# A hybrid encoder block: two thirds of the convolution's taps as ScalarE products, and six pairs instead of four by seven products in four groups

## The chip, the core and the metric

The kernel runs on one core of one Trainium2 chip. A core has a matrix engine (TensorE, PE in the profile, with its weight loads as PEld), a vector engine (VectorE, DVE), an activation engine (ScalarE, ACT), a general engine (GpSimd, POOL) and a queue engine (SyncE, SP) that here only issues transfers. Each works through its own instructions in order, and they wait for each other by semaphores. The metric is device time in microseconds (us) of one execution; the times given are medians.

## What is computed

One layer of a streaming encoder on 256 rows of 4096 columns, all in float32:

```python
proj = rms_norm(h, norm_in_g) @ w_in             # 4096 -> 7 x 2048: q, k, v, z_a, a_c, g_c, z_c
y_a  = rms_norm(chunked_attention(q, k, v, table)) * silu(z_a)
u    = a_c * sigmoid(g_c)                        # 256 rows x 2048 channels
u    = causal_depthwise_conv(u, w_dw) + b_dw     # 31 taps, one filter for each channel
y_c  = rms_norm(silu(layer_norm(u)) @ w_pw + b_pw) * silu(z_c)
h    = h + concat(y_a, y_c) @ w_out
h    = h + sigmoid(rms_norm(h) @ w_ple_gate + b) * (p @ w_ple)
out  = rms_norm(h)
```

The change touches the depthwise convolution and the products that make a_c, g_c, q, k and v.

## The kernel before

**Precision.** Each float32 matrix is split into a high part (a cast to fp32r) and a low part (the rest), and each product of two blocks is three: high by high, low by high, high by low. For a weight tile of 128 x 1024 that means one cast on ScalarE (line 204: `wh`, `uh`) and one subtraction on VectorE (line 205: `wl`, `ul`). Weight tiles arrive in five buffers, the parts of plain tiles have three buffers each, those of sums two.

**A group.** `mixed_product` makes two blocks of 512 output columns for both halves of the 256 rows, four accumulators, over the 4096 inner rows, which are sixteen pairs of 128-row blocks. A *plain* pair takes 2 blocks x 2 row halves x 2 column blocks x 3 = 24 products of 128x512. A pair *by seven products* (a Strassen-Winograd step) takes 7 x 3 = 21, but needs sums of its weight blocks. They are made by VectorE: two for `ua` (lines 467 and 468) and two for `ub` (474 and 475), and both results are split like weights. A pair marked `*` does just that. A pair marked `+` has its `ua` summed by two transfers, one on SP's queue and an accumulating one on GpSimd's (lines 420 and 421), and keeps only 474 and 475 on VectorE. The left side needs sums of the activations too ("combinations"). Those of pairs 8 and 10 are made while a group runs, in `more_combinations`, and are used by sevens 8 and 10.

The order of a group's pairs is a list written out by hand:

```python
early     = units("1 3 5 0+ 7 9 2+ 11 13 4+ 15 8 6+ 10 12 14")       # four sevens
early_six = units("1 3 5 0+ 7 2* 9 4+ 11 6* 13 8+ 15 10* 12 14")     # six sevens
```

After the last seven, VectorE adds up the helper accumulators (lines 513 to 516); after the last pair it scales the four accumulators into `z` (line 538), and TensorE transposes the result.

**Order of the groups.** conv 0, conv 1 (each makes a_c and g_c for 512 channels), q0/k0, v0/v1, attention 0, conv 2, q1/k1, attention 1, conv 3, q2/k2, q3/v2, attention 2, layer norm, k3/v3, attention 3, and then the pointwise, output and embedding products. Conv 2 and conv 3 use `early_six`; conv 1, q0/k0, v0/v1, q1/k1 and q2/k2 use `early`; q3/v2 has five sevens.

**The convolution.** At the end of each conv group the gated values are transposed into `uT` (four blocks of 128 channels x 256 rows), and `glu_conv` puts the taps into a queue of small tasks, `later`: for each of the four blocks, 31 instructions on VectorE, each of which takes `uT` shifted by some rows, multiplies by one column of weights and adds to `cv` (line 724; the unshifted one, with the offset, is line 720). The shifted tap k covers 226 + k columns, so 241 on average. After each pair of a group, `fill(n)` takes n tasks from the queue, by the lists `early_fills` (64 in all) and `six_fills` (63).

**What sets the order on an engine.** The instructions are traced in program order. Then they are put into each engine's queue by that order among those that are ready; so an instruction that needs nothing may come much earlier than it was traced. `queued_behind(made)` puts what is traced inside it behind the given instruction on the same engine. `recent` holds the newest pair of cast and subtraction. Tiles of one tag share a fixed number of slots: "hd" has five of 128 x 1024 (`uT`, the bias tables, `kT`, v), "stage" two, "act" eight.

Of the kernel before, what the change touches and what calls it, by code (L numbers as in the profile page):

```python
# [10 lines left out]
F32 = mybir.dt.float32  # L11
F32R = mybir.dt.float32r
AF = mybir.ActivationFunctionType
ALU = mybir.AluOpType
AX = mybir.AxisListType

P = 128
# [8 lines left out]
def hybrid_block(  # L26
# [305 lines left out]
    early_five = units("1 3 5 0+ 7 9 2+ 11 4* 13 6+ 15 8* 10 12 14")  # L332
    early_six = units("1 3 5 0+ 7 2* 9 4+ 11 6* 13 8+ 15 10* 12 14")

    early_fills = (5, 6, 1, 5, 6, 1, 5, 6, 1, 5, 6, 1, 2, 5, 5, 4)
    six_fills = (6, 6, 1, 5, 1, 5, 1, 5, 1, 5, 1, 5, 1, 6, 7, 7)
    norm = units("1 3 5 7 9 11 0+ 13 2* 15 4+ 8 6* 10 12 14")
    norm_fills = (7, 8, 8, 8, 6, 4, 2, 3, 2, 3, 2, 2, 0, 6, 5, 5)
    final = units("1 0* 3 2* 5 4* 6* 7 8* 9 10* 12* 11 13 14 15")
# [378 lines left out]
    def conv_tap(cv, uT, i, b, k):  # L718
# [4 lines left out]
        else:  # L723
# [2 lines left out]
                cv[:, i, PAD - k :], ALU.mult, ALU.add,  # L726
            )

    def more_combinations(pair):

        if pair in (7, 9):
            c = (pair + 1) // 2
            xS[2 * c] = act.tile([P, 2, 2, T], F32R, tag="act", name="comb_x"), 0
            later.extendleft(reversed(combinations(c)))

    def glu_conv(c):
        if c == 0:
            sg, gate = scaled_pair(
                w_in0, o_a, o_g - o_a, first, r_x, (1,), begin=first_pairs
            )  # L740
        else:
            sg, gate = scaled_pair(
                w_in0, o_a + c * NB, o_g - o_a,
                *((early, r_x, early_fills) if c == 1 else (early_six, r_x, six_fills)),
                ahead=more_combinations if c == 2 else None,
            )
        for h in range(NH):
            nc.scalar.activation(gate[:, h, :], gate[:, h, :], AF.Sigmoid)
            tt(sg[:, h, :], sg[:, h, :], gate[:, h, :], ALU.mult)
        uT = spool.tile([P, 4, T], F32, tag="hd", name="uT", bufs=5)  # L750
        for pair in range(2):
            pt = tmp_psum()
            for i in range(2):
                for h in range(NH):
                    b = 2 * pair + i
                    nc.tensor.transpose(
                        pt[:, i * T + h * P : i * T + (h + 1) * P],
                        sg[:, h, b * P : (b + 1) * P],
                        ident,
                    )  # L760
            nc.scalar.copy(
                uT[:, 2 * pair : 2 * pair + 2, :], pt.rearrange("q (i t) -> q i t", t=T)
            )
        cv = act.tile([P, 4, T], F32, tag="act", name="cv")
        for i in range(4):
            for k in reversed(range(TAPS)):
                later.append(partial(conv_tap, cv, uT, i, 4 * c + i, k))
        conv.append(cv)


# [184 lines left out]
    def heads(*parts, order=None, fills=early_fills, **kw):  # L955

        cols = [o + g * NB for o, g in parts]
        tiles = scaled_pair(
            w_in0, cols[0], cols[1] - cols[0], order or early, r_x, fills,
            homes=[home if o == o_v else dict(tag="stage") for o, _ in parts], **kw  # L960
        )
        for (o, g), t in zip(parts, tiles):
            if o == o_v:
                vs[g] = t
            else:
                (queries_of if o == o_q else keys_of)(g, t)
# [6 lines left out]

    n_g = H // GH
    assert n_g == CW // NB == 4
    glu_conv(0)
    glu_conv(1)
    load_bias(0)
    heads((o_q, 0), (o_k, 0))
    heads((o_v, 0), (o_v, 1))  # L980
    attention(0)
    glu_conv(2)
    load_bias(1)
    heads((o_q, 1), (o_k, 1))
    attention(1)
    glu_conv(3)
    load_bias(2)
    heads((o_q, 2), (o_k, 2))
    heads((o_q, 3), (o_v, 2), order=early_five)
    attention(2)  # L990
    layer_norm_swish()
    load_bias(3)
# [359 lines left out]
```

## Time and profile before

| | us |
|---|---|
| median of three runs | 2029.58 |
| lowest and highest | 2027.98, 2029.75 |
| the profiled execution | 2028.23 |
| its span, first to last instruction | 2026.5 |
| PE, DVE, ACT busy in the span | 2010.8, 1903.4, 1215.0 |
| granted TensorE clock | 0.998 |

The profile is one execution. Its page lists busy times, the chain of work that ended last and the costliest groups of instructions; the trace behind it can be asked for stretches of time, single lines and the order of instructions. A group's row gives line, engine, operation, the tile written and those read, shape and count, then busy time and mean duration in ns, and after the second bar the idle time just ahead of these instructions and what ended it. Products overlap in the record (each lasts about 0.39 us but the next starts earlier), so a busy PE isn't PE at its full rate: the distance between their starts tells more than the busy share.

### The profile page before, as it was taken

The numbers are of one execution on the slowest core, as the hardware profiler recorded it, in microseconds if no ns is written. First come the engines' busy times: TensorE is split into PE (matmuls) and PEld (weight loads), VectorE is DVE, ScalarE is ACT, GpSimd is POOL, SyncE is SP. The second block draws the span as 40 slices with busy tenths as digits, with TensorE's granted clock in tenths as the row PEclk, the third lists the DMA queues.
The fourth block names the chain that finished last, engine by engine and source line by source line (L and its number), as shares of the span: only waits on it lengthen the run. The fifth ranks groups of instructions, "written<-read, shape, count | busy, mean of one in ns | idle before, by whom it ended". The sixth has DMA issues, their size and how long they took to land.

```text
span 2026.5 us, 26195 instructions
## 1 busy us (share of the span) xinstructions
PE 2010.8 (99%) x9073; PEld 1654.4 (82%) x9073; DVE 1903.4 (94%) x2708; ACT 1215.0 (60%) x1583; POOL 46.9 (2%) x50
## 2 busy tenths in 40 slices
PE   9999999999999999999999999999999999999997
PEld 7888888888888888788888888888888888888876
DVE  7999999889999997888899999999999999999998
ACT  7655545655655555776556556666665666655555
POOL 0000000000000000000000000000000000000000
PEclk9999999999999999999999999999999999999999
DMA  8787878678678867456666666676666656666765
GB/s 295 222 238 234 255 217 250 177 247 240 188 221 246 252 198 241 156 177 209 196 208 207 208 204 211 208 239 210 203 211 197 208 194 201 208 218 207 231 207 180
DMA packets 171168, 436.70 MB, mean 215 GB/s; under 512 B 13966, under 2 KB 17182, under 8 KB 171034
## 3 DMA queue, kind: packets, MB, share of 16 engines
q1 hardware_dynamic: 161952, 417.93, 63.9%
q0 software_dynamic: 8432, 16.25, 4.8%
q8 instruction: 71, 1.16, 0.2%
q10 hardware_dynamic: 650, 0.84, 0.1%
q14 instruction: 63, 0.52, 0.1%
HBM read 430.77 MB, written 4.19 MB: 215 GB/s over the span
## 4 chain that ended last, share of the span: by engine, by line
PE 95%; DVE 3%; issue 1%; ACT 1%; DMA 0%; POOLq 0%; POOL 0%; ACTq 0%; SPq 0%; DVEq 0%
PE acc L385 73%; PE acc_P L385 17%; PE tmp_ps L170 1%; DVE cv L724 1%; PE acc L229 1%; DVE wl L205 1%; PE tmp_ps L893 0%; PE tmp_ps L877 0%; PE tmp_ps L911 0%; PE tmp_ps L916 0%; PE acc L373 0%; ACT wh L204 0%; PE tmp_ps L892 0%; DVE ul L205 0%; DMA xin<-in_x_dram 0%
## 5 line engine op out<-in xcount | busy, mean ns | idle before, releaser
L385 PE MATMUL acc<-wh,big_t 128*128 128x512 f32 x4154 | 1283.3, 391 | 0.6 <-DVE y_c L1043 0.4
L204 ACT CAST wh<-wt 128x1024 fp32r<-128x1024 f32 (+1 forms) x737 | 710.1, 974 | 523.3 <-PE acc L385 364.3
L385 PEld LDWEIGHTS acc<-wh,big_t 128*128 128x128 f32 x4154 | 777.0, 188 | 160.8 <-DVE y_c L1043 0.9
L205 DVE TENSOR_TENSOR wl<-wt,wh 128x1024 fp32r<-128x1024 f32 (+1 forms) x737 | 817.4, 1122 | 39.9 <-ACT wh L204 33.6
L385 PE MATMUL acc<-wl,big_t 128*128 128x512 f32 x2077 | 801.9, 391 | 0.1
L385 PEld LDWEIGHTS acc<-wl,big_t 128*128 128x128 f32 x2077 | 389.5, 188 | 82.5 <-DVE wl L205 1.8
L204 ACT CAST uh<-ua 128x1024 fp32r<-128x1024 f32 x174 | 182.9, 1052 | 91.1 <-DVE ua L468 46.3
L205 DVE TENSOR_TENSOR ul<-ua,uh 128x1024 fp32r<-128x1024 f32 x174 | 212.0, 1219 | 9.6 <-ACT uh L204 8.1
L724 DVE SCALAR_TENSOR_TENSOR cv<-uT,dw,cv 128x250 f32<-128x250 f32 (+19 forms) x480 | 203.6, 464 | 1.1
L385 PE MATMUL acc_P<-uh,big_t 128*128 128x512 f32 x528 | 161.8, 392 | 0.0
L204 ACT CAST uh<-ub 128x1024 fp32r<-128x1024 f32 x92 | 96.8, 1052 | 95.5 <-DVE ub L475 79.2
L205 DVE TENSOR_TENSOR ul<-ub,uh 128x1024 fp32r<-128x1024 f32 x92 | 112.2, 1220 | 6.7 <-ACT uh L204 5.6
L385 PEld LDWEIGHTS acc_P<-uh,big_t 128*128 128x128 f32 x528 | 98.0, 188 | 23.2 <-ACT uh L204 3.7
L385 PE MATMUL acc_P<-ul,big_t 128*128 128x512 f32 x264 | 101.3, 392 | 0.0
L467 DVE TENSOR_TENSOR ua<-wt 128x512 f32<-128x512 f32 x102 | 69.9, 685 | 17.3 <-DMA wt<-in_w_in_dram 10.7
L385 PE MATMUL acc<-uh,big_t 128*128 128x512 f32 x266 | 82.5, 390 | 0.0
L385 PE MATMUL acc_P<-wh,big_t 128*128 128x512 f32 x266 | 82.1, 389 | 0.0
L468 DVE TENSOR_TENSOR ua<-wt 128x512 f32<-128x512 f32 x102 | 69.6, 683 | 4.3 <-DMA wt<-in_w_in_dram 3.6
L385 PE MATMUL acc_P<-uh,comb_t 128*128 128x512 f32 x228 | 70.1, 390 | 0.1
L475 DVE TENSOR_TENSOR ub<-ub,wt 128x512 f32<-128x512 f32 x92 | 63.0, 685 | 0.8
L474 DVE TENSOR_TENSOR ub<-ua,wt 128x512 f32<-128x512 f32 x92 | 62.9, 683 | 0.3
L385 PEld LDWEIGHTS acc_P<-ul,big_t 128*128 128x128 f32 x264 | 49.3, 188 | 12.5 <-DVE ul L205 2.0
(243 smaller groups left out, 1485.5 us busy)
## 6 DMA issues: line engine op xcount, KB each, us to landing
wt<-in_w_in_dram SPq DMA_DIRECT2D x416, 512.0 KB, 4.5
wt<-in_w_out_dram SPq DMA_DIRECT2D x128, 512.0 KB, 4.3
wt<-in_w_ple_gate_dram SPq DMA_DIRECT2D x128, 512.0 KB, 4.2
wt<-in_w_pw_dram SPq DMA_DIRECT2D x32, 512.0 KB, 4.8
ua<-in_w_in_dram SPq DMA_DIRECT2D x31, 512.0 KB, 4.3
ua<-in_w_in_dram POOLq DMA_DIRECT2D x31, 512.0 KB, 8.7
wt<-in_w_in_dram SPq DMA_DIRECT2D x31, 256.0 KB, 2.8
hc<-in_x_dram SPq DMA_DIRECT2D x8, 512.0 KB, 4.7
```

Of the source, the lines that this page charges most:

```text
L170: nc.tensor.transpose(pt[:, i * T + h * P : i * T + (h + 1) * P], src[:, h, b] if len(src.shape) == 4 else src[:, h, b * P : (b + 1) * P], ...
L204: nc.scalar.copy(wh[:, :kc, :], wt[:, :kc, :]),
L205: nc.vector.tensor_tensor(wl[:, :kc, :], wt[:, :kc, :], wh[:, :kc, :].bitcast(F32), ALU.subtract),
L229: nc.tensor.matmul(acc, a, b[:, k, :], start=kb == 0 and kind == 0, stop=kb == kblocks - 1 and kind == 2,)
L385: nc.tensor.matmul(banks[name], a, b, start=name not in begun, stop=final and ends[name] == n and kind == 2 and not (left and name in "P2 ...
L467: plus(ua[:, 0], w0[:, 0], w0[:, 1])
L468: plus(ua[:, 1], w0[:, 1], w1[:, 1])
L474: plus(ub[:, 0], ua[:, 0], w1[:, 1])
L475: plus(ub[:, 1], ub[:, 0], w1[:, 0])
L724: nc.vector.scalar_tensor_tensor(cv[:, i, PAD - k :], uT[:, i, : T + k - PAD], dw[:, b, k : k + 1], cv[:, i, PAD - k :], ALU.mult, ALU.add,)
```

## The change

Four parts, all between conv 1 and attention 2:

- q0/k0, v0/v1, q1/k1 and q2/k2 use `early_six` in place of `early`: two more sevens each, and three `+` and three `*` in place of four `+`.
- Of each convolution's 30 shifted taps, every third stays as it was (k = 0, 3, ..., 27; four VectorE instructions each). The other twenty become a *wide tap*: four products on ScalarE, one for each block, into a tile `wu`, and one addition on VectorE for all four blocks. The products are queued behind the newest weight cast (`recent[0]`). `wu` has two tiles in turn, which are taken from the "hd" or "stage" slots, newly for each group.
- A convolution is now 64 tasks (4 + 20 wide + 40 narrow) in place of 124, taken by shorter lists: 37 for `early_fills`, 36 for `six_fills`.
- The combinations for pairs 8 and 10 are made in conv 1's group in place of conv 2's.

```diff
-    early_fills = (5, 6, 1, 5, 6, 1, 5, 6, 1, 5, 6, 1, 2, 5, 5, 4)
-    six_fills = (6, 6, 1, 5, 1, 5, 1, 5, 1, 5, 1, 5, 1, 6, 7, 7)
+    early_fills = (3, 3, 1, 3, 3, 1, 3, 3, 1, 3, 3, 1, 1, 3, 3, 2)
+    six_fills = (3, 3, 1, 3, 1, 3, 1, 3, 1, 3, 1, 3, 1, 3, 3, 3)
...
+    weighted = []
+
+    def weighted_in(*homes):
+
+        weighted[:] = homes
+
+    def wide_tap(cv, uT, b, k):
+
+        if not hasattr(weighted[0], "rearrange"):
+            weighted[:] = [spool.tile([P, 4, T], F32, name="wu", **kw) for kw in weighted]
+        weighted.append(weighted.pop(0))
+        n = T + k - PAD
+        with queued_behind(recent[:1]):
+            for i in range(4):
+                nc.scalar.activation(
+                    weighted[0][:, i, :n], uT[:, i, :n], AF.Identity, scale=dw[:, b + i, k : k + 1]
+                )
+            tt(cv[:, :, PAD - k :], cv[:, :, PAD - k :], weighted[0][:, :, :n], ALU.add)
...
-                ahead=more_combinations if c == 2 else None,
+                ahead=more_combinations if c == 1 else None,
...
-        for i in range(4):
-            for k in reversed(range(TAPS)):
-                later.append(partial(conv_tap, cv, uT, i, 4 * c + i, k))
+        def taps(k, blocks):
+            later.extend(partial(conv_tap, cv, uT, i, 4 * c + i, k) for i in blocks)
+
+        taps(PAD, range(4))
+        for k in range(0, PAD, 3):
+            for n in range(2):
+                later.append(partial(wide_tap, cv, uT, 4 * c, k + 1 + n))
+                taps(k, (2 * n, 2 * n + 1))
...
+    stage, six = dict(tag="stage"), dict(order=early_six, fills=six_fills)
     glu_conv(0)
+    weighted_in(home, home)
     glu_conv(1)
     load_bias(0)
-    heads((o_q, 0), (o_k, 0))
-    heads((o_v, 0), (o_v, 1))
+    weighted_in(home, home)
+    heads((o_q, 0), (o_k, 0), **six)
+    weighted_in(stage, stage)
+    heads((o_v, 0), (o_v, 1), **six)
     attention(0)
+    weighted_in(home, home)
     glu_conv(2)
     load_bias(1)
-    heads((o_q, 1), (o_k, 1))
+    weighted_in(home, home)
+    heads((o_q, 1), (o_k, 1), **six)
     attention(1)
+    weighted_in(home, home)
     glu_conv(3)
     load_bias(2)
-    heads((o_q, 2), (o_k, 2))
-    heads((o_q, 3), (o_v, 2), order=early_five)
+    weighted_in(home, home)
+    heads((o_q, 2), (o_k, 2), **six)
+    weighted_in(stage, home)
+    heads((o_q, 3), (o_v, 2), order=early_five, fills=six_fills)
```

## The prediction

> **What bounds the kernel now.** The chain that ended last comes first (page, part 4), then its pieces in time order inside one group.
>
> ```profile
> PE 95%; DVE 3%; issue 1%; ACT 1%; DMA 0%; POOLq 0%; POOL 0%; ACTq 0%; SPq 0%; DVEq 0%
> ```
> ```profile
> 384.08 6.12 PE acc L385 x27
> 390.20 2.04 PE acc_P L385 x9
> 392.24 1.36 PE acc L385 x6
> ```
> TensorE holds the chain, and inside a group it stops for nothing: these 42 products follow each other within 9.52 us, 0.2267 us each. A plain pair (24 products) is 5.44 us, a pair by seven products (21) 4.76 us, so each pair turned saves 0.68 us. The cost lands elsewhere, so next come the stretches of the eight groups that the change touches (ends read off the evictions on L538): conv 1, q0/k0, v0/v1, conv 2, q1/k1, conv 3, q2/k2, q3/v2. Columns: length, then busy time of PE, PEld, DVE, ACT, POOL.
>
> ```profile
> 101.70:187.40 85.70, 85.53 (x381) 70.52 (x380) 85.68 (x141) 44.39 (x49) 4.88 (x4) 1.00 0.82 238
> 187.40:271.20 83.80, 83.80 (x380) 69.46 (x379) 83.80 (x140) 43.38 (x48) 5.18 (x5) 1.00 0.84 245
> 271.20:357.50 86.30, 86.30 (x387) 71.56 (x386) 85.95 (x144) 45.34 (x52) 4.87 (x4) 1.00 0.79 232
> 357.50:447.60 90.10, 90.10 (x417) 74.09 (x416) 73.50 (x102) 54.82 (x82) 3.65 (x3) 1.00 0.70 213
> 447.60:533.20 85.60, 85.55 (x386) 70.67 (x385) 85.55 (x141) 45.60 (x52) 5.17 (x5) 1.00 0.82 240
> 533.20:625.40 92.20, 92.20 (x431) 76.09 (x430) 85.14 (x134) 57.39 (x87) 3.66 (x3) 1.00 0.69 208
> 625.40:711.10 85.70, 85.68 (x387) 70.73 (x386) 85.65 (x142) 45.71 (x52) 5.18 (x5) 1.00 0.82 240
> 711.10:796.50 85.40, 85.40 (x387) 70.92 (x386) 80.22 (x113) 45.75 (x53) 3.95 (x4) 1.00 0.77 231
> ```
> VectorE is full in five of eight, ScalarE about half idle in all. The same view for the taps alone shows what kind of full this is:
>
> ```profile
> 187.40:271.20 83.80, 32.86 (x80) 1.00 0.84 245
> 357.50:447.60 90.10, 4.53 (x10) 1.00 0.70 213
> ```
> The fills release 64 entries in q0/k0, yet 80 taps run there, and conv 2 finds 10 left. Taps need only what VectorE already has, so they run early wherever it has room: that fullness is elastic, and TensorE keeps its pace beside it. In sum VectorE idles 694.80 - 665.48 = 29.3 us over the eight.
>
> **The change part by part.** Prices on VectorE, grouped by shape over the eight stretches, and the pitch at which they follow each other:
>
> ```profile
> L205 DVE TENSOR_TENSOR wl<-wt,wh 128x1024 fp32r<-128x1024 f32 x219 | 264.4, 1220 | 9.9 <-ACT wh L204 9.5
> L205 DVE TENSOR_TENSOR ul<-ua,uh 128x1024 fp32r<-128x1024 f32 x74 | 90.3, 1220 | 7.9 <-ACT uh L204 6.7 <-PE acc L385 1.2
> L475 DVE TENSOR_TENSOR ua<-ua,wt 128x512 f32<-128x512 f32 x37 | 25.4, 687 | 0.2
> L205 DVE TENSOR_TENSOR wl<-wt,wh 128x512 fp32r<-128x512 f32 x37 | 25.4, 686 | 0.4 <-ACT wh L204 0.3
> L474 DVE TENSOR_TENSOR ua<-ua,wt 128x512 f32<-128x512 f32 x37 | 25.4, 686 | 0.0
> L538 DVE SCALAR_TENSOR_TENSOR z<-acc,r_x,z 128x512 f32<-128x512 f32 x32 | 22.0, 747 | 3.8 <-PE acc L385 3.8
> ...
> L724 DVE SCALAR_TENSOR_TENSOR cv<-uT,dw,cv 128x241 f32<-128x241 f32 x16 | 7.4, 466 | 0.1
> ```
> ```profile
> 305.15 2.38 DVE L205 TENSOR_TENSOR wl<-wt,wh 128x1024 fp32r<-128x1024 f32 x2
> 307.42 0.49 DVE L724 SCALAR_TENSOR_TENSOR cv<-uT,dw,cv 128x244 f32<-128x244 f32 x1
> ```
> Two subtractions advance VectorE by 2.27 us, 1.135 each where the mean is 1.22. So an instruction costs its mean less about 0.085: 1.135, 0.60 for 512 columns, 0.66 for an eviction, 0.38 for an average tap.
>
> *Removed and added products.* Four groups go from four to six sevens: 8 x 0.68 = **5.44 us off TensorE**.
>
> *VectorE for the sevens.* Plain pair: 2 x 1.135 = 2.27. A "+" pair: 0.60 + 3 x 1.135 + 2 x 0.60 = 5.2; a "*" adds its own two sums on L467 and L468, 6.4. Four "+" and twelve plain are 48.0; three "+", three "*" and ten plain 57.5. So +9.5 a group, +38 in all.
>
> *Taps.* 320 of 480 leave: -320 x 0.38 = -122. In their place come 80 additions over four blocks, 4 x 241 = 964 columns on average. No row has that shape; it lies between 512 columns (0.60) and the 1024 of L205 (1.135). By the slope between them it is 1.07, which I take: +86. Net -36, and VectorE asks +2 us in all, of 29.3 idle, of which TensorE takes 5.4 away. On average it fits.
>
> *ScalarE.* 320 products with a column of scales, 241 columns on average. Nearest rows:
>
> ```profile
> L204 ACT CAST wh<-wt 128x1024 fp32r<-128x1024 f32 x604 | 627.9, 1052 | 440.3 <-PE acc L385 316.4 <-DVE cv L724 27.6 <-issue 25.9
> ...
> L204 ACT CAST wh<-wt 128x512 fp32r<-128x512 f32 x133 | 82.6, 621 | 83.0 <-PE acc L385 47.9 <-issue 20.3 <-ACT wh L204 7.8
> L156 ACT ACTIVATE big_t<-tmp_ps,prm 128x256 fp32r<-128x256 f32 x64 | 27.7, 470 | 4.1 <-DVE big_t L157 2.5 <-PE tmp_ps L170 1.6
> L534 ACT ACTIVATE z<-z,r_x 128x512 f32<-128x512 f32 x30 | 20.6, 718 | 23.3 <-DVE z L514 21.9 <-DVE z L516 1.4
> ```
> The casts give 0.84 ns a column, so L534 less 271 columns is 0.49; L156, from PSUM, says 0.46. I take 0.49, with the same overlap 0.40 a product, 1.6 us for a wide tap; L534 unshortened (0.63) is the far end, 2.5 us. The sum is 128 us, and the sevens add 8 x 1.5 of casts: 140 us into 694.8 - 382.4 = 312 us of idle. Hidden on average, if the pieces fit the gaps.
>
> The Trainium skill speaks against this move: "ScalarE: Activation LUTs", under Rules for kernel authors, sends multiplications to VectorE, not ScalarE. By it the taps stay and the sevens ask 38 us of a VectorE with 29.3 idle, over budget; by the rows ScalarE's idle time is free, so the move stands.
>
> *What stops being elastic.* Each product is queued behind the newest weight cast, so taps no longer run ahead: the fills now pace them. A six group releases 36 entries, about 11 wide and 21 narrow taps and four offset taps (12 wide, 24 narrow in v0/v1). VectorE then asks 57.5 + 5.0 (four helper sums at 0.60, four evictions at 0.66) + 11.8 + 8.0 + 1.3 = 83.6 us, in v0/v1 84.4: 335.2 over the four. TensorE needs their lengths less 5.44, 336.0. That is 99.8%, with nothing to fill a hole. Worse in the middle: from the first seven to the last (six sevens, five plain, fills 3 and 1) TensorE needs 55.8, VectorE 46.2 + 14.0 of taps = 60.2. The missing 4.4 us must come from its lead. How large that is, conv 3 shows, as six-seven already; the last subtraction of a seven on VectorE, and the product on TensorE that first reads it, in its first and fifth seven:
>
> ```profile
> 555.71 1.22 DVE L205 TENSOR_TENSOR wl<-wt,wh 128x1024 fp32r<-128x1024 f32 x1
> ...
> 598.48 1.22 DVE L205 TENSOR_TENSOR wl<-wt,wh 128x1024 fp32r<-128x1024 f32 x1
> ```
> ```profile
> 560.37 0.39 PE L385 MATMUL acc<-wl,big_t 128*128 128x512 f32 x1
> ...
> 601.17 0.39 PE L385 MATMUL acc<-wl,big_t 128*128 128x512 f32 x1
> ```
> The lead is 560.37 - 556.93 = 3.4 us, then 601.17 - 599.70 = 1.5. So 3.4 of the 4.4 are covered and 1.0 is not; the last fill (1.8) may come after the last subtraction that counts. Between 0 and the full 1.0 plus the end's helper sums (2.4) I take 0.7 a group, the near end, because three plain pairs refill the lead at each start: **2.8 us given back**.
>
> *Waits.* Additions wait for products; behind them on VectorE stand the subtractions that TensorE needs. Products wait for one of two buffers, freed by the addition before last; behind them stand the casts. Both are inside the 0.7. In conv 2 and conv 3 the buffers share slots with attention's tiles and start late; 16.6 and 7.1 us of VectorE idle cover it. Two combinations move from conv 2 to conv 1, which still has room (48.0 + 5.0 + two gate products 1.2 + some 19 of taps and 4 of combinations, 77 of 85.7): 0. Four "+" fewer take four sum loads off SP's queue and four off POOL's; the four groups gain twelve "*", whose sums on VectorE wait for both weight tiles: 0, DMA has 0% of the chain; without that cover the wait is VectorE's, and adds to C.
>
> Sum: 2028.23 (profiled, span 2026.5) - 5.44 + 2.8 = 2025.6; the median shown lies 1.35 higher, so **2027.0**.
>
> **Rivals.** *A, forecast*: as above, 2027.0. Against it: the 0.7 rests on a lead measured with elastic taps.
>
> *B, all arrives*: the lead covers the middle, 2029.58 - 5.44 = 2024.1. For: q0/k0 at 83.80 of 83.80 loses nothing. Against: 99.8% without filler.
>
> *C, slower: products in front of casts.* ScalarE around conv 3's fifth seven, and the taps on VectorE in the first and last of the four cycles (plain and seven) between the two leads above, 22 in all:
>
> ```profile
> 596.42 1.05 ACT L204 CAST wh<-wt 128x1024 fp32r<-128x1024 f32 x1
> 598.69 2.00 ACT L204 CAST wh<-wt 128x1024 fp32r<-128x1024 f32 x2 [1.22 <-issue]
> ```
> ```profile
> 558.40:568.60 10.20, 2.94 (x7) 1.00 0.56 174
> ...
> 589.00:599.20 10.20, 2.11 (x5) 1.00 0.63 206
> ```
> The gap before the next plain pair's cast is 1.22, a wide tap 1.6: 0.4 late at each seven, 2.3 a group. And conv 3's lead fell 0.5 a cycle at 22 / 4 x 0.38 = 2.1 us of taps; four entries ask 2.4, so 0.8 a cycle, 4.5 over 5.5 cycles against 3.4 of lead. Together 3.4 us a group, 13.6 in all: 2037.7. It decides once a cycle's products and additions outrun the lead before the last two sevens. Against: leads in q0/k0 hold while VectorE is full.
>
> *D, VectorE is the bound.* It is full in five stretches; if it sets their time, its +2 us is the result: 2031.6. The Trainium skill's "Perfetto Trace Analysis", under Identifying the Most-Contended Engine, would have it so: it takes occupancy as a fair measure for VectorE. Against: conv 2 at 73.50 of 90.10, TensorE no faster.
>
> That the sevens don't come is no case: the order lists fix them.
>
> **How the numbers follow.** Chances: A 0.40, B 0.24, C 0.22, D 0.14. A measurement tells about 0.2% (4.1 us) from no change. Faster than 2025.5: B and a little of A, 0.27. Slower than 2033.6: C and the upper part of D, 0.26. The rest 0.47. The range 2023.8 to 2037.0 holds A, B and D and most of C; its lower end is the whole saving.
>
> **What would show it.** In the profile after: eight fewer groups of three products in the four stretches, each 1.4 us shorter (right) or unchanged (D); 320 ScalarE products near 0.49 and 80 additions near 1.16; gaps in TensorE's product rows at the first plain pair behind a seven (C) or none (B); VectorE idle on ScalarE products inside the four groups where it has none now. The forecast is wrong if those gaps sum to under 1 us or over 8.

## The result and the profile after

| us | before | after |
|---|---|---|
| median | 2029.67 (6 runs) | 2044.82 (6 runs) |
| lowest and highest | 2027.98, 2029.95 | 2042.51, 2047.15 |
| profiled execution, its span | 2028.23, 2026.5 | 2047.15, 2045.4 |
| granted TensorE clock | 0.998 | 0.995 |

The ratio is 1.0077, 95% interval [1.0065, 1.0088]: the change costs about 15 us. The forecast was 2027.0, and the time lies above the whole range. The profiled execution after is the slowest of the six, 2.3 us above their median. The page after, busy times first, then the head of the chain that ended last, then four rows of the groups (busy us, mean ns, and behind the second bar the idle time just ahead of these instructions).

```profile
PE 2019.0 (99%) x9049; PEld 1648.9 (81%) x9049; DVE 1909.0 (93%) x2524; ACT 1343.6 (66%) x1919; POOL 42.2 (2%) x46
...
PE 60%; DVE 4%; issue 1%; ACT 1%; DMA 1%; POOLq 0%; POOL 0%; ACTq 0%; DVEq 0%; SPq 0%
...
L743 ACT ACTIVATE wu<-uT,dw 128x227 f32<-128x227 f32 (+19 forms) x320 | 133.2, 489 | 0.2
...
L746 DVE TENSOR_TENSOR cv<-cv,wu 128x908 f32<-128x908 f32 (+9 forms) x80 | 92.6, 1157 | 9.4 <-ACT wu L743 8.1
L467 DVE TENSOR_TENSOR ua<-wt 128x512 f32<-128x512 f32 x114 | 78.1, 685 | 15.8 <-DMA wt<-in_w_in_dram 9.9
...
L724 DVE SCALAR_TENSOR_TENSOR cv<-uT,dw,cv 128x226 f32<-128x226 f32 (+9 forms) x160 | 70.4, 460 | 0.1
```

The prices are those of the prediction: a product takes 489 ns (0.49 was taken), an addition 1157 (1.155). What is new is that VectorE waits 8.1 us for products. The fall of TensorE's share of the chain, from 95% to 60%, can't be read as time lost: the shares of this row add up to 67% only, those of before to 100%, and the 18.9 us between the two spans are 1%. The eight groups, conv 1 to q3/v2, with borders at each group's first eviction on L538 (length, then busy time of PE, PEld, DVE, ACT, POOL, clock):

```profile
97.60:182.80 85.20, 85.20 (x381) 70.56 (x380) 78.95 (x104) 59.81 (x92) 6.11 (x5) 1.00 0.86 251
182.80:269.70 86.90, 86.90 (x384) 70.33 (x382) 85.04 (x106) 63.45 (x98) 2.87 (x3) 1.00 0.70 215
269.70:356.90 87.20, 86.63 (x386) 70.09 (x385) 84.25 (x106) 65.38 (x103) 4.12 (x4) 1.00 0.72 220
356.90:451.60 94.70, 92.05 (x410) 72.68 (x409) 85.08 (x115) 64.50 (x110) 3.19 (x3) 0.98 0.66 197
451.60:540.60 89.00, 86.76 (x377) 70.17 (x376) 85.61 (x107) 65.15 (x99) 5.17 (x5) 0.98 0.77 230
540.60:634.10 93.50, 93.50 (x439) 76.29 (x438) 85.78 (x119) 69.05 (x120) 2.44 (x2) 1.00 0.67 197
634.10:724.50 90.40, 86.91 (x373) 69.02 (x373) 86.53 (x109) 66.08 (x101) 5.17 (x5) 0.98 0.75 227
724.50:810.70 86.20, 86.20 (x386) 70.70 (x385) 81.70 (x99) 58.77 (x87) 3.95 (x4) 1.00 0.80 232
```

With the same borders the kernel before has 85.9, 85.4, 86.4, 90.0, 85.7, 92.1, 85.8 and 85.2, in sum 696.5; after it is 713.1, so 16.6 of the 18.9 us between the spans lie here. VectorE idles 40.2 us in these eight groups where it idled 29.3. The four groups that should have become 1.4 us shorter each went from 343.3 to 353.5, conv 2 from 90.0 to 94.7. The gaps of TensorE, counted from one product's start to the next over 0.227 us, sum to 23.9 us in the whole span before and 48.6 after: +24.7, less the 5.44 saved, is about the 18.9. In conv 2, 5.5 us of them stand in its first 10 us, where before has 0.6: there TensorE waits for the evictions of v0/v1 (0.95 us) and for the subtractions behind them (1.45 us), so most of that loss belongs to a group's end, too.

The two longest of these gaps stand at the ends of q1/k1 and q2/k2. The first, on TensorE (start, length, instruction, in brackets the idle time before and what ended it), then on VectorE and ScalarE:

```profile
532.94 1.98 PE L385 MATMUL acc<-wh,big_t 128*128 128x512 f32 x8
537.09 1.91 PE L385 MATMUL acc<-wl,big_t 128*128 128x512 f32 x4 [2.18 <-DVE wl L205]
```
```profile
530.16 1.15 DVE L746 TENSOR_TENSOR cv<-cv,wu 128x956 f32<-128x956 f32 x1 [0.33 <-ACT wu L743]
531.23 0.68 DVE L513 TENSOR_TENSOR z<-acc_P,z 128x512 f32<-128x512 f32 x1
...
533.78 1.15 DVE L746 TENSOR_TENSOR cv<-cv,wu 128x960 f32<-128x960 f32 x1
534.85 0.68 DVE L516 TENSOR_TENSOR z<-acc_P,z 128x512 f32<-128x512 f32 x1
535.45 0.45 DVE L724 SCALAR_TENSOR_TENSOR cv<-uT,dw,cv 128x238 f32<-128x238 f32 x1
535.82 2.35 DVE L205 TENSOR_TENSOR wl<-wt,wh 128x1024 fp32r<-128x1024 f32 x2
```
```profile
526.36 1.27 ACT L743 ACTIVATE wu<-uT,dw 128x240 f32<-128x240 f32 x3
527.53 1.04 ACT L204 CAST uh<-ua 128x1024 fp32r<-128x1024 f32 x1
528.47 2.05 ACT L743 ACTIVATE wu<-uT,dw 128x239 f32<-128x239 f32 x5
530.40 2.00 ACT L204 CAST wh<-wt 128x1024 fp32r<-128x1024 f32 x2
```

The casts of the first plain pair behind the last seven are done at 532.4. Their subtractions could follow at once, but start at 535.82: two additions, the four helper sums and the taps between them fill VectorE without a hole from 530.16. Eight products run between 526.4 and 530.5, at the very end of the group, and their additions come due when the helper sums do. TensorE waits 2.18 us for `wl`.

### The profile page after: what moved, and what is told of

It is laid out like the page before. It is cut to its first block, busy times and chain, and to the rows that moved or that the text cites. A ratio compares the mean times of both kernels' runs of the same rounds, so it can differ in the third digit from the quotient of the medians.

```text
span 2045.4 us, 26278 instructions
## 1 busy us (share of the span) xinstructions
PE 2019.0 (99%) x9049; PEld 1648.9 (81%) x9049; DVE 1909.0 (93%) x2524; ACT 1343.6 (66%) x1919; POOL 42.2 (2%) x46
## 4 chain that ended last, share of the span: by engine, by line
PE 60%; DVE 4%; issue 1%; ACT 1%; DMA 1%; POOLq 0%; POOL 0%; ACTq 0%; DVEq 0%; SPq 0%
PE acc L385 45%; PE acc_P L385 12%; DVE wl L205 1%; PE acc L229 1%; PE tmp_ps L170 1%; DVE ul L205 0%; DMA wt<-in_w_ple_gate_dram 0%; ACT uh L204 0%; DVE hc L184 0%; ACT wh L204 0%; DVE cv L826 0%; PE acc L373 0%; DMA wt<-in_w_in_dram 0%; DVE ub L474 0%; PE tmp_ps L917 0%
## 5 line engine op out<-in xcount | busy, mean ns | idle before, releaser
L385 PE MATMUL acc<-wh,big_t 128*128 128x512 f32 x4042 | 1250.7, 392 | 2.6 <-DVE z L538 1.0
L385 PEld LDWEIGHTS acc<-wh,big_t 128*128 128x128 f32 x4042 | 756.8, 188 | 162.2 <-DVE z L538 3.1
L385 PE MATMUL acc<-wl,big_t 128*128 128x512 f32 x2021 | 777.1, 394 | 6.3 <-DVE wl L205 6.2
L385 PEld LDWEIGHTS acc<-wl,big_t 128*128 128x128 f32 x2021 | 379.6, 188 | 89.3 <-DVE wl L205 11.0
L204 ACT CAST uh<-ua 128x1024 fp32r<-128x1024 f32 x190 | 199.6, 1051 | 82.5 <-DVE ua L468 56.8
L205 DVE TENSOR_TENSOR ul<-ua,uh 128x1024 fp32r<-128x1024 f32 x190 | 231.5, 1219 | 12.4 <-ACT uh L204 11.6
L743 ACT ACTIVATE wu<-uT,dw 128x227 f32<-128x227 f32 (+19 forms) x320 | 133.2, 489 | 0.2
L746 DVE TENSOR_TENSOR cv<-cv,wu 128x908 f32<-128x908 f32 (+9 forms) x80 | 92.6, 1157 | 9.4 <-ACT wu L743 8.1
L467 DVE TENSOR_TENSOR ua<-wt 128x512 f32<-128x512 f32 x114 | 78.1, 685 | 15.8 <-DMA wt<-in_w_in_dram 9.9
L468 DVE TENSOR_TENSOR ua<-wt 128x512 f32<-128x512 f32 x114 | 77.9, 683 | 2.4 <-DMA wt<-in_w_in_dram 1.7
L724 DVE SCALAR_TENSOR_TENSOR cv<-uT,dw,cv 128x226 f32<-128x226 f32 (+9 forms) x160 | 70.4, 460 | 0.1
```

Source lines behind the costliest of these rows:

```text
L204: nc.scalar.copy(wh[:, :kc, :], wt[:, :kc, :]),
L205: nc.vector.tensor_tensor(wl[:, :kc, :], wt[:, :kc, :], wh[:, :kc, :].bitcast(F32), ALU.subtract),
L385: nc.tensor.matmul(banks[name], a, b, start=name not in begun, stop=final and ends[name] == n and kind == 2 and not (left and name in "P2 ...
L467: plus(ua[:, 0], w0[:, 0], w0[:, 1])
L468: plus(ua[:, 1], w0[:, 1], w1[:, 1])
L724: nc.vector.scalar_tensor_tensor(cv[:, i, PAD - k :], uT[:, i, : T + k - PAD], dw[:, b, k : k + 1], cv[:, i, PAD - k :], ALU.mult, ALU.add,)
```

## The experiments

Each theory is named as the expectations name it. Theory 1: the order on VectorE; taps are paced and no longer elastic, so additions and helper sums stand in front of subtractions. Theory 2: products stand in front of casts on ScalarE (half of rival C). Theory 3: VectorE simply has too much to do. Lengths of groups (first eviction to first eviction) are from the trace of each run, which is one execution; medians and ratios are of all; the four are q0/k0, v0/v1, q1/k1, q2/k2, which take 343.3 us before and 353.5 after.

| run | median, us | ratio to before | the four | conv 2 | conv 3 |
|---|---|---|---|---|---|
| e1 sevens alone | 2034.7 | 1.0023 [1.0013, 1.0033] | 342.4 | 92.9 | 93.7 |
| e2 taps alone | 2033.43 | 1.0018 [1.0009, 1.0028] | 342.0 | 94.1 | 93.2 |
| e3 additions that need no product | 2029.74 | 1.0002 [0.9992, 1.0011] | 341.1 | 91.5 | 92.2 |
| e4 fills first | 2069.92 | 1.0198 [1.0183, 1.0213] | 364.4 | 98.0 | 99.1 |
| e5 no tie to the cast | 2030.24 | 1.0006 [0.9996, 1.0015] | 342.6 | 91.6 | 91.4 |
| e6 light ends | 2041.1 | 1.0058 [1.0042, 1.0075] | 346.5 | 96.9 | 94.4 |
| e7 five sevens alone | 2032.97 | 1.0020 [1.0010, 1.0029] | 342.3 | 92.0 | 93.8 |
| e8 taps alone, fills of 44 | 2030.52 | 1.0008 [0.9999, 1.0018] | 343.2 | 91.3 | 92.8 |
| e9 no tie, five sevens | 2032.32 | 1.0014 [1.0005, 1.0023] | 342.5 | 91.4 | 93.0 |
| e10 no tie, four sevens | 2033.63 | 1.0026 [1.0017, 1.0036] | 342.3 | 94.5 | 92.9 |
| e11 no tie, no narrow taps | 2028.08 | 0.9995 [0.9986, 1.0005] | 339.3 | 90.9 | 93.3 |
| e12 no tie, six sevens in two groups | 2033.55 | 1.0024 [1.0015, 1.0034] | 342.6 | 96.2 | 91.5 |
| e13 no tie, fills of 44 and 42 | 2048.86 | 1.0100 [1.0085, 1.0115] | 358.1 | 92.4 | 95.7 |
| e14 fills of 44 and 42 | 2053.49 | 1.0120 [1.0105, 1.0135] | 361.5 | 91.8 | 94.6 |
| e15 one cast back | 2038.19 | 1.0044 [1.0029, 1.0059] | 344.2 | 95.1 | 93.1 |
| e16 no tie, four sevens, fills of 44 | 2028.67 | 1.0000 [0.9990, 1.0009] | 342.5 | 90.9 | 92.8 |
| e17 no taps, six sevens | 2022.7 | 0.9974 [0.9965, 0.9982] | 336.4 | 90.8 | 93.0 |
| e18 no taps, four sevens | 2030.47 | 1.0008 [0.9999, 1.0017] | 342.0 | 90.6 | 93.6 |

### The halves of the change

e1 has the sevens with the taps and fills as they were before:

```diff
-        taps(PAD, range(4))
-        for k in range(0, PAD, 3):
-            for n in range(2):
-                later.append(partial(wide_tap, cv, uT, 4 * c, k + 1 + n))
-                taps(k, (2 * n, 2 * n + 1))
+        for i in range(4):
+            for k in reversed(range(TAPS)):
+                later.append(partial(conv_tap, cv, uT, i, 4 * c + i, k))
```

> The sevens alone: all taps back on VectorE as in the kernel before, with its fills; the four groups keep six sevens. Theory 1 (order: with products and additions, a group's taps are no longer elastic, and on VectorE they and the helper sums stand ahead of the last pairs' subtractions): the taps are elastic again, so no long stall at the end of a group; the 38 us that VectorE gets too much of push the last taps into the layer norm's stretch: 2026 to 2034. Theory 2 (ScalarE: products ahead of the weight casts make TensorE wait): no products, so the whole saving arrives, about 2024. Theory 3 (VectorE simply has more work than time): 665 + 38 = 703 us in 689, over by 14: 2038 to 2044.

e2 has the taps with four sevens:

```diff
-    stage, six = dict(tag="stage"), dict(order=early_six, fills=six_fills)
+    stage, six = dict(tag="stage"), {}
```

> The taps alone: ScalarE products and wide additions as in the changed kernel, but the four groups keep four sevens. Theory 1 (order at the end of a group, where VectorE is short of time): with four sevens VectorE has some 10 us a group to spare, so 2028 to 2033, with the first stalls of the changed kernel gone. Theory 2 (products ahead of casts): the 320 products are all there, so most of the loss stays: 2040 or more. Theory 3 (work): VectorE has 36 us less to do than before: 2029 to 2030.

They measure 2034.7 and 2033.4: +5.0 and +3.7. The halves add to 8.7 us where the whole costs 15.2, so the two disturb each other. Theory 1 is nearest in both, but its ranges end 0.7 and 0.4 us below. With the sevens alone, VectorE is busy 696.4 of the 701.2 us of the eight groups; the four become 0.9 us shorter, not 5.44, and conv 2 and conv 3 grow to 92.9 and 93.7. The taps alone leave the four groups as they were; most of their loss lies in conv 2. Its row and that of q1/k1 in e2:

```profile
353.80:447.90 94.10, 92.41 (x419) 73.36 (x419) 82.44 (x111) 65.78 (x111) 2.44 (x2) 1.00 0.63 193
447.90:533.20 85.30, 85.30 (x382) 70.66 (x381) 77.38 (x95) 61.53 (x95) 6.39 (x6) 1.00 0.87 253
```

VectorE has 8 us of room in q1/k1 with four sevens. Conv 2, which before had 10 taps and 73.40 us of VectorE, is given 82.44.

### Who waits for whom

In e3 the wide additions read `uT` in place of `wu`. The products are still made and still tied to the casts, but nobody waits for them.

```diff
-            tt(cv[:, :, PAD - k :], cv[:, :, PAD - k :], weighted[0][:, :, :n], ALU.add)
+            tt(cv[:, :, PAD - k :], cv[:, :, PAD - k :], uT[:, :, :n], ALU.add)
```

> As the changed kernel, but the wide additions read the convolution's input instead of the products, so the convolution's values are others; ScalarE still makes all 320 products, queued as before, and nothing waits for them. VectorE's work is the same. Theory 1 (taps lost their elasticity): the taps may run early again, and the saving mostly arrives: 2024 to 2030. Theory 2 (products ahead of casts): nothing changes on ScalarE: 2040 to 2046. Theory 3 (VectorE's work): the same work: 2040 to 2046.

2029.74, the time of the kernel before, in theory 1's range. ScalarE does all that it did, and VectorE too, yet the 15 us are gone. Theory 2 and theory 3 by themselves fall as the cause of the 15 us: what costs is that additions wait for products.

e5 takes away the tie that makes the products late:

```diff
-        with queued_behind(recent[:1]):
+        with queued_behind(()):
```

> As the changed kernel, but the products aren't queued behind the newest weight cast; only the two buffers hold them back. Theory 1 (the taps' place in VectorE's queue, since they lost their elasticity): they may run ahead again, by two wide taps at most, so part of the loss goes: 2030 to 2038. Rival (the queueing behind the casts protects the casts): products now get in front of casts and it grows worse: 2046 or more.

2030.24, at the lower end of theory 1's range: this one line carries 14.6 of the 15.2 us (14.4 by the ratios). The end of q1/k1 in e5, on VectorE:

```profile
522.69 1.22 DVE L205 TENSOR_TENSOR wl<-wt,wh 128x1024 fp32r<-128x1024 f32 x1
523.83 0.68 DVE L513 TENSOR_TENSOR z<-acc_P,z 128x512 f32<-128x512 f32 x1
524.43 1.15 DVE L746 TENSOR_TENSOR cv<-cv,wu 128x960 f32<-128x960 f32 x1
...
527.07 1.22 DVE L205 TENSOR_TENSOR wl<-wt,wh 128x1024 fp32r<-128x1024 f32 x1
528.20 0.68 DVE L516 TENSOR_TENSOR z<-acc_P,z 128x512 f32<-128x512 f32 x1
528.80 0.46 DVE L724 SCALAR_TENSOR_TENSOR cv<-uT,dw,cv 128x238 f32<-128x238 f32 x1
529.18 1.22 DVE L205 TENSOR_TENSOR wl<-wt,wh 128x1024 fp32r<-128x1024 f32 x1
```

The same helper sums and an addition stand here, but subtractions come between them. The free products do wait for their two tiles, with casts behind them, as the prediction feared; the trace of e5 (101.7 to 812 us) has it at 19.8 us, against 3.7 us that additions wait:

```profile
ACT wu L743 <- DVE cv L746: 19.8, 19, 2.4
...
DVE cv L746 <- ACT wu L743: 3.7, 5, 1.2
```

ScalarE, a quarter idle in these groups, can bear it. VectorE beside six sevens can't bear the 8.1 us that it waits after; beside four it waits 10.7 us for products in e2, and the four groups lose nothing. So the sum of these waits doesn't give the cost by itself: what stands behind them does.

e15 ties the products to the cast ahead of the newest one:

```diff
+        older[:] = recent[:1]
         recent[:] = made
...
-        with queued_behind(recent[:1]):
+        with queued_behind(older):
```

> The change with one word different: products are queued behind the cast ahead of the newest one, instead of behind the newest. If what costs is that products must wait for a cast that is itself waiting for an accumulator or for VectorE's sum, most of the 14.6 us goes: 2030 to 2034, and no half clock. If any tie to a cast bunches the products late in a group, most of it stays: 2039 to 2045.

2038.19, between the two expectations: one cast less of delay takes 6.6 of the 14.6 us away. The cost grows with how late the products are; the newest cast isn't all of it. The four groups are back at 344.2 us; what is left lies in conv 2, conv 3 and q3/v2 (95.1, 93.1 and 87.5, in e5 91.6, 91.4 and 85.3), in conv 2 mostly in its first 10 us (4.3 us of gaps).

### The fills

The fills say where in the order the taps stand. e4 puts them first in the six groups, e6 only lightens their ends:

```diff
-    six_fills = (3, 3, 1, 3, 1, 3, 1, 3, 1, 3, 1, 3, 1, 3, 3, 3)
+    six_fills = (6, 6, 6, 3, 1, 3, 1, 3, 1, 3, 1, 2, 0, 0, 0, 0)
```

> As the changed kernel, but with the fills of a six group moved to its start: 6, 6, 6, 3, 1, 3, 1, 3, 1, 3, 1, 2, 0, 0, 0, 0 (36 again). Theory 1: the stalls of 2.3 us ahead of the last pairs of q1/k1 and q2/k2, and the half clock behind each (1.6 us), go: 8 to 10 us less, 2034 to 2038. Theory 2: the same products, some now in front of the first casts: 2043 to 2048. Theory 3: the same work: 2043 to 2046.

```diff
-    six_fills = (3, 3, 1, 3, 1, 3, 1, 3, 1, 3, 1, 3, 1, 3, 3, 3)
+    six_fills = (4, 4, 2, 3, 1, 3, 1, 3, 1, 3, 1, 3, 1, 1, 1, 1)
```

> As the changed kernel, with lighter fills behind the last three pairs of a six group: 4, 4, 2, 3, 1, 3, 1, 3, 1, 3, 1, 3, 1, 1, 1, 1 (33 in place of 36; the three taken out flow on to later groups). Theory 1: the stalls of 2.3 us ahead of the last pairs of q1/k1 and q2/k2 and the half clock behind them shrink or go: 2034 to 2040. Rival (only the sum of VectorE's work counts, not its place): the work is the same: 2043 to 2046.

e4 takes 2069.92, 25 us more, where all three theories had at most 2048: the stall moves from the ends to sevens in the first two thirds of a group and grows there. In q0/k0 TensorE waits 2.02 us for the cast of a sum, at 210.1; on VectorE an addition stands between the two steps of that sum (206.58 to 208.98). So the place in the queue counts, as theory 1 says, but theory 1 had these places better than the end, and they are worse. e6 does what theory 1 says where it was applied: q1/k1 and q2/k2 fall from 89.0 and 90.4 to 86.3 and 86.1. But what it takes from them comes back in conv 2 (96.9) and conv 3 (94.4), and 2041.1 is left, above theory 1's range and below its rival's. Neither of the two other places tried is better for the whole.

e8 is e2 with heavier fills, 44 entries in place of 37 in conv 1 and the four groups, so that conv 2 begins with an empty queue:

```diff
-    early_fills = (3, 3, 1, 3, 3, 1, 3, 3, 1, 3, 3, 1, 1, 3, 3, 2)
+    early_fills = (3, 3, 2, 4, 4, 1, 4, 4, 1, 4, 4, 1, 1, 3, 3, 2)
...
-    stage, six = dict(tag="stage"), dict(order=early_six, fills=six_fills)
+    stage, six = dict(tag="stage"), {}
```

> The new taps alone, as in the run of the taps alone, but with 44 tasks a group in place of 37 where there are four sevens, so that conv 1, q0/k0 and v0/v1 finish the first two convolutions and conv 2 finds none left. Theory 1: conv 2's extra 4 us go, since nothing paced is left to stand in front of its sums, and the groups with four sevens have room: 2028 to 2030.5. Rival (the products as such cost, wherever they are): 2033 or more.

2030.52, at the edge of theory 1's range, and conv 2 is back at 91.3. e16 is the same without the tie:

> New taps alone, products free of the casts, four sevens in the four groups and fills of 44. Against the same kernel with fills of 36 (2033.6) conv 2 should fall from 94.5 to 91 us: 2029.5 to 2031, as the kernel with the tie and these fills did (2030.5). If conv 2 stays above 94, the fills are not what makes the new taps dear and that earlier reading falls.

2028.67, 0.8 us below the range, with conv 2 at 90.9 and a ratio of 1.0000: with four sevens and enough fills, the new taps cost nothing that can be told, and with four sevens the tie doesn't either (by the ratios 1.6 us from e16 to e8, -1.6 from e10 to e2). So the tie is dear only beside the six sevens: with it, going from four sevens to six (e2 to after) takes the ratio from 1.0018 to 1.0077; without it (e10 to e5), from 1.0026 to 1.0006.

### Where the 5.44 us stay without the tie

e5 has neither the 15 us nor the gain. e7 is e1 with five sevens (`early_five`), e9 to e12 vary e5.

> Half of the sevens, without the new taps: the four groups get five sevens (the order of q3/v2) in place of four, the taps are those of before. TensorE saves 4 x 0.68 = 2.7 us, VectorE gets some 5 us more a group, 21 in all, of 29 idle, and its taps stay elastic. Theory 1: nothing paced stands in front of the sums, so most of it arrives: 2027 to 2028.5. Rival (each added seven brings a wait of its own, as in the run of the sevens alone, where eight cost 10.4 us of stalls): 4 x 1.3 - 2.7: 2031 to 2033.

> The products are free of the casts here, as in the run without that line (2030.24), and each of the four early groups makes five of its sixteen pairs by seven products instead of six; the fills keep the change's places. Against the kernel before that is 2.7 us of TensorE saved instead of 5.44. If what is left over in the run without the line is VectorE's work in these groups (335 of 336 us), four more plain pairs give VectorE some 15 to 17 us back and most of the 2.7 us arrives: 2026.5 to 2028.5. If each seven brings a wait of its own for its tile or its cast, about as large as what it saves, a seven less changes nothing: 2029.5 to 2030.5.

> The products are free of the casts and the four early groups keep the four sevens that they have before: only the taps are changed. Nothing is saved on TensorE, and VectorE is given 36 us of work back over the taps alone. If the new taps are free once the products are not tied to the newest cast: 2029 to 2030, the time before within 0.1 %, and no gap of TensorE over 0.5 us in conv 2 and conv 3 beyond those before. If the wide additions cost something of their own (four blocks become ready at once, and late): 2031 to 2032, with the gaps in conv 2 and conv 3.

> The products are free of the casts, and six sevens stand in q1/k1 and q2/k2 alone; q0/k0 and v0/v1 keep four. TensorE saves 2.72 us against the kernel before. In the run without the line the last two of these groups took 85.5 us each with six sevens, the first two 85.5 and 86.2. If sevens are dear only where VectorE is crowded (q0/k0 and v0/v1, ahead of which taps pile up): 2026.5 to 2028.5. If every seven pays about its own saving in waits: 2029.5 to 2030.5.

e7 takes 2032.97, which the intervals don't tell from the six sevens of e1; it lies in the rival's range, not in theory 1's. e9 (2032.32), e10 (2033.63) and e12 (2033.55) lie above both of their expectations. Without the tie, fewer sevens are slower, not faster: from six to four the time rises by 3.4 us, and the rise lies in conv 2 (91.6 to 94.5) and conv 3 (91.4 to 92.9), not in the four groups, which take 342 to 343 us with four sevens as with six. So here the sevens bring their own groups nothing. That a conv 2 which has taps left is sensitive to what stands ahead of it is my reading. In e10 ScalarE waits there for a weight transfer:

```profile
413.08 2.15 ACT L204 CAST wh<-wt 128x1024 fp32r<-128x1024 f32 x2 [2.22 <-DMA wt<-in_w_in_dram]
```

e12 has three such waits, e5 none. Why the transfer is late with four sevens ahead isn't settled.

e11 is e5 without the narrow shifted taps, e13 is e5 with full fills, e14 the same with the tie:

```diff
-                taps(k, (2 * n, 2 * n + 1))
+                later.extend([lambda: None] * 2)
```

> As the run without the line that ties products to casts (2030.24), and the 160 narrow shifted taps of VectorE are left out, so that the convolution's values differ; their places in the queue stay, empty. VectorE has 70.4 us less to do, and the order of all else is the same. If the 5.44 us of six sevens didn't arrive there because VectorE's helper sums and subtractions stand behind taps, they arrive now: 2024 to 2025.5, and the gaps from conv 1 to q3/v2 sum to that of before or less. If sevens have waits of their own (for a tile, a cast or an accumulator), the gaps stay: 2028.5 to 2030.

```diff
-    early_fills = (3, 3, 1, 3, 3, 1, 3, 3, 1, 3, 3, 1, 1, 3, 3, 2)
-    six_fills = (3, 3, 1, 3, 1, 3, 1, 3, 1, 3, 1, 3, 1, 3, 3, 3)
+    early_fills = (3, 3, 2, 4, 4, 1, 4, 4, 1, 4, 4, 1, 1, 3, 3, 2)
+    six_fills = (4, 4, 1, 4, 1, 4, 1, 4, 1, 4, 1, 4, 1, 4, 2, 2)
```

> Six sevens in the four groups, products free of the casts, and fills of 44 and 42 entries a group in place of 36, so that the taps of conv 0 and conv 1 are done when conv 2 begins. If the fills are what is left of the loss, conv 2 falls from 91.6 to about 90 us and conv 3 from 91.4 to about 91, and the time to 2027 to 2028.5, below the kernel before. If the sevens need the room on VectorE that the extra fills take (q0/k0 and v0/v1 go from about 102 us of VectorE records to 106), these groups grow by what conv 2 gives back: 2029.5 to 2031.

> The change with the fills of 44 and 42, the tie to the newest cast kept. If the tie makes products and additions late whenever six sevens crowd VectorE, more fills per group make it worse there and better in conv 2 and conv 3: 2042 to 2050, with the gaps in q1/k1 and q2/k2 no smaller than 5.2 and 7.4 us. If the loss in the change came from taps left over for conv 2 and conv 3: 2030 to 2035.

e13 misses both of its expectations by far: 2048.86. The four groups of e5, and q1/k1 and conv 2 of e13:

```profile
182.80:268.20 85.40, 84.90 (x376) 68.82 (x375) 85.20 (x108) 62.61 (x96) 2.74 (x3) 1.00 0.72 219
268.20:354.40 86.20, 85.91 (x387) 70.62 (x386) 84.82 (x108) 66.18 (x104) 3.65 (x3) 1.00 0.77 228
...
446.00:531.50 85.50, 85.50 (x380) 70.00 (x379) 84.76 (x108) 64.25 (x99) 4.10 (x5) 1.00 0.77 231
...
622.90:708.40 85.50, 85.50 (x380) 69.96 (x379) 84.70 (x108) 64.68 (x99) 3.95 (x4) 1.00 0.78 238
```
```profile
362.10:454.50 92.40, 90.35 (x414) 73.05 (x413) 73.57 (x97) 56.52 (x87) 3.65 (x3) 1.00 0.74 218
454.50:544.70 90.20, 87.36 (x377) 70.20 (x376) 87.46 (x112) 67.98 (x107) 3.96 (x4) 0.98 0.67 207
```

VectorE is busy 339.5 of the 342.6 us of the four in e5. Six more entries a group (two wide and four narrow in q1/k1) make it 87.5 in q1/k1, and the group grows to 90.2. That is not an elastic fullness: VectorE's work alone is now longer than the 85.5 us of the group in e5, and waits come on top. The longest of them in q1/k1 is for the cast of a sum:

```profile
531.23 0.69 DVE L475 TENSOR_TENSOR ua<-ua,wt 128x512 f32<-128x512 f32 x1
```
```profile
531.54 1.27 ACT L743 ACTIVATE wu<-uT,dw 128x245 f32<-128x245 f32 x3
532.72 1.03 ACT L204 CAST uh<-ua 128x1024 fp32r<-128x1024 f32 x1
```
```profile
533.80 1.10 PE L385 MATMUL acc_P<-uh,comb_x 128*128 128x512 f32 x2 [2.00 <-ACT uh L204]
```

The sum is there at 531.92, but three products stand in front of its cast, which starts 0.8 us later. So theory 2, which e3 rules out for the 15 us of the change, is a part of the loss here. In e16 fills of 44 beside four sevens leave the group at 85.3. Sevens and taps each fit, both together don't. e14 (2053.49) has the tie on top of it, above both of its ranges.

e11 lands at 2028.08, just under what the sevens' own waits would give and far from what VectorE's work would, which then seemed ruled out. The last two runs undo that. They are e5 without any shifted tap, and so without ScalarE's products as well, e17 with six sevens, e18 with four:

```diff
-                later.append(partial(wide_tap, cv, uT, 4 * c, k + 1 + n))
-                taps(k, (2 * n, 2 * n + 1))
+                later.extend([lambda: None] * 3)
```

> Six sevens in the four groups, and all 240 shifted taps' instructions of conv 0 to conv 3 on VectorE (160 narrow, 80 wide) and the 320 products left out, so that the convolution's values differ; their places in the queue stay, empty. VectorE has some 160 us less to do. If VectorE's room was all that kept the 5.44 us of TensorE away, this kernel is 5 to 5.5 us below the one with four sevens and no taps, at 2022 to 2024.5 us. If each seven has a wait of its own, for its cast, its sum or an accumulator, whatever VectorE has to do, it is 1.5 to 4 us below it.

> The same without shifted taps, with four sevens in the four groups as before the change. TensorE's work is that of the kernel before. If the taps cost the kernel before nothing, as its gaps of 0.2 to 0.7 us in these groups say: 2027 to 2029.5, within 0.1 % of it.

2022.7 against 2030.47, 7.8 us apart. e17 lies in its first range, e18 1.0 us above its own, and that isn't explained. The four groups, in e17 and in e18:

```profile
182.40:266.30 83.90, 83.90 (x376) 69.52 (x375) 67.55 (x76) 47.54 (x54) 3.95 (x4) 1.00 0.78 233
266.30:351.10 84.80, 84.80 (x384) 70.36 (x383) 65.20 (x70) 47.35 (x54) 3.66 (x3) 1.00 0.75 226
...
441.90:525.70 83.80, 83.80 (x375) 69.42 (x374) 67.85 (x76) 48.66 (x55) 3.97 (x4) 1.00 0.77 236
...
618.70:702.60 83.90, 83.90 (x376) 69.51 (x375) 67.73 (x76) 48.87 (x55) 3.96 (x4) 1.00 0.77 236
```
```profile
182.60:267.80 85.20, 85.20 (x382) 70.55 (x381) 58.31 (x62) 44.28 (x50) 5.17 (x5) 1.00 0.82 241
267.80:354.00 86.20, 86.20 (x390) 71.53 (x389) 55.92 (x56) 44.19 (x50) 4.87 (x4) 1.00 0.79 231
...
444.60:529.90 85.30, 85.30 (x382) 70.64 (x381) 58.50 (x62) 45.69 (x51) 5.18 (x5) 1.00 0.84 245
...
623.50:708.80 85.30, 85.30 (x382) 70.68 (x381) 58.50 (x62) 45.73 (x51) 5.17 (x5) 1.00 0.83 246
```

336.4 against 342.0: the sevens' 5.44 us are there, 5.6 by these rows, once the taps are gone, and a seven has no wait of its own worth speaking of, whatever e7 seemed to say. (The profiled execution of e17 took 2026.77, 4 us above its median; the four groups are those of the trace. Where the other 2.2 of the 7.8 us lie, it doesn't show.) With the wide taps (e11) 339.3, with all taps (e5) 342.6: each part takes about 3 us back. In e11 VectorE is not full in the four (312.3 us busy of 339.3), so it isn't occupancy alone. What else it is there, no run separates: the longest gap of these groups in e11, 0.9 us at 507.3, follows a wait of VectorE of 0.93 us for a weight tile. Since e17 takes work from ScalarE as well as from VectorE, it is e13 that speaks for VectorE, busy 87.5 us for a group that took 85.5, and e16, where ScalarE makes all products and nothing is lost. None of the versions that compute the layer beats the kernel before; e16 equals it.

## Why the prediction was wrong

The step that failed is *Waits*: "Additions wait for products; behind them on VectorE stand the subtractions that TensorE needs. … Both are inside the 0.7", and with it the sum's last term, 2.8 us given back. The wait was named rightly and given nothing of its own. Additions wait 8.1 us for products after, and the tie that makes the products late carries 14.6 us of the result (after less e5), where VectorE has no hole to take it up. The 2.8 us given back measure 15.6: the four groups are 10.2 us longer, not 5.44 shorter. The forecast was to be wrong if the gaps came to more than 8 us; in the four groups alone they are 16.6 where before has 1.6.

Point by point:

- *Added sevens, 5.44 us off TensorE*: right, 5.6 by the four rows of e17 and e18. All of it arrives only without taps.
- *VectorE for the sevens, +38 us*: right. In the four groups 268.3 (e17) less 231.2 (e18) is 37.1.
- *Prices of product and addition*: right, 489 ns and 1157 ns. VectorE's sum over the eight groups, +2: right where the tie is off, 669.1 in e5 against 667.2.
- *335.2 us asked of VectorE in the four groups, 336.0 that TensorE leaves*: the second is right, 336.4 in e17. The first was 1.3% short, 339.5 in e5. That is small, but it crosses the line: 3.1 us more than there is, not 0.8 less. At 99.8% the forecast should not have rested on which side the sum came out.
- *Two combinations moved to conv 1, and twelve `*` that wait for weight tiles: 0*: right. Conv 1 takes 85.2 where it took 85.9, and L467 waits 9.9 us for its tiles after and 10.7 before.
- *0.7 a group*: wrong. The middle of the group, for which it was worked out, is not where most was lost; the longest gaps of q1/k1 and q2/k2 stand at the group's end (4.0 and 3.7 of their 5.2 and 7.4 us), where the prediction let helper sums and last fills cost nothing beyond it.
- *Conv 2 and conv 3, slots: 0*: ScalarE idles only 0.2 us ahead of all 320 products, so slots that come free late don't show as a wait; the work left over does. Fills of 36 and 37 leave conv 2 seven or eight wide additions and 14 to 16 narrow taps, where it had 10 taps. With four sevens that is worth 2 to 3 us by e2 against e8 (by the ratios, or by the medians 2033.43 and 2030.52), with conv 2 at 94.1 and 91.3. The prediction counted the entries that a group releases, and not those that are left.

*The rivals.* C came nearest in time (2037.7), and its second half, the lead on VectorE outrun, is close to what happens. Its sign is there, too: the gap at 537.09 stands at the first plain pair behind a seven, the last one. Its first half, products in front of casts, falls with e3 as the cause of the 15 us, and shows where the fills are heavier (0.8 us in e13). D gave 2031.6 as VectorE's bound: that is near what is left once the tie is off (2030.24). By the rule of the Trainium skill's "Perfetto Trace Analysis", under Identifying the Most-Contended Engine, VectorE's occupancy was the sign to trust: before the change the trace speaks against it, since the four groups last 342.0 with no taps (e18) and 343.3 with them; in e13 it agrees.

What the fullness of before was, e18 and e17 say: with four sevens VectorE needs 58.5 of 85.3 us in q1/k1, and the old taps filled the rest without being in the way. The prediction saw that this elasticity goes ("the fills now pace them") and priced its loss by averages. Why the new taps can't run ahead even without the tie (e5 runs as many of them in each of the four groups as after, but for one) was not tried; I argue from the code that a narrow tap on a block of `cv` must follow the wide addition ahead of it, and that one its products and one of two tiles.

## What to carry to other kernels

An engine that is full of work which can run at any time has room for waits; the same share of work that stands in a fixed order, or waits for another engine, has hardly any, and in this kernel its waits reached the bottleneck. Before moving work to an idle engine, ask where in the receiving and in the returning queue each piece will stand: putting a producer behind the newest instruction of its queue delayed a consumer that stood ahead of the critical work, and cost 14.6 us where 5.44 were to be saved. When a queue of fillers is shortened, count what is left at its end, not only what each stage takes out.

## What the runs showed of the hardware

TensorE's clock fell to half behind some gaps of about 2 us. The gap of after at 534.5 and the stretch behind it (length; PE, PEld, DVE, ACT, POOL; clock):

```profile
534.50:537.00 2.50, 0.42 (x2) 0.00 (x0) 2.50 (x5) 2.35 (x4) 0.00 (x0) 1.00 1.04 368
537.00:541.00 4.00, 3.91 (x10) 3.12 (x11) 4.00 (x6) 1.04 (x1) 1.22 (x1) 0.57 0.78 230
```

Behind the gap TensorE makes 10 products in 3.9 us of work where 17 fit at 0.227 us: about 1.6 us more, nearly as much as the gap. The record of granted clocks has it at 0.5 for 3.41 us each time, at 363.2, 537.3 and 721.6. The kernel before, e5 and e6 have it at 0.5 only in the last 10 us or so, as every run does. The Trainium skill's "TensorE: Matmul & The Clock Gate", in Part 1, gives the half clock to an idle window of about 3.4 us, and the full one back after a busy window as long. The trace agrees with the second, 3.41 us, but not with the first: idle stretches of about 2.2 us were enough at 537.3 (2.18 in the row of TensorE above) and 721.6, and two of 0.95 and 1.45 us close together at 363.2. Nor does the length of a stretch decide by itself. In e13 an idle stretch of 2.00 us (at 533.8, shown above) brought the half clock, and this one of 2.05 us did not:

```profile
719.73 0.73 PE L385 MATMUL acc_P<-uh,comb_x 128*128 128x512 f32 x2 [2.05 <-ACT uh L204]
```

Nor did one of 2.27 us in e4, at 599.4. What else decides isn't tried. The three half clocks cost some 4.8 of the 18.9 us of the profiled execution, at 1.6 each.
